# A hybrid decoder layer on one core: two output-projection weight tiles loaded earlier, two converted later, and other queues for the first inputs and the last store

## The chip, the cores and the metric

The kernel runs on one core of one Trainium2 chip. The time is device microseconds (us) of one execution; the kernel before has a median of 1073.84 us in three runs (1071.54 to 1075.19). A core has a matrix engine (TensorE, PE in the profile, with PEld for its weight loads), a vector engine (VectorE, DVE), a scalar engine (ScalarE, ACT), a general engine (GpSimd, POOL) and SyncE (SP), which only starts transfers. Each engine takes its instructions in the order in which they stand in its own program, and waits where an operand isn't ready; what stands behind a waiting instruction waits with it. A transfer is started by an instruction on SP, POOL or ACT (SPq, POOLq, ACTq in the profile) and is carried out by 16 DMA engines beside them.

## The reference

One layer of a decoder runs over 512 prompt tokens and 8 x 4 sample tokens that share the weights, all in float32, with a model width of 1024 and an FFN width of 2816:

```python
x = layer_norm(ALPHA * x + 0.5 * swiglu(x, ffn1_wg, ffn1_wu, ffn1_wd), ln1_g, ln1_b)
proj = x @ w_in                                  # 1024 -> 3328
...                                              # token shift; r, w, k, v, kk, a per head; gate g
def step(s, inp):                                # RWKV-7, 8 heads of size 64, one token at a time
    r_t, w_t, k_t, v_t, kk_t, a_t = inp
    sa = einsum("bhij,bhj->bhi", s, -kk_t)
    s = s * w_t[:, :, None, :] + sa[..., None] * (kk_t * a_t)[:, :, None, :] + v_t[..., None] * k_t[:, :, None, :]
    return s, einsum("bhij,bhj->bhi", s, r_t)
...                                              # o: group norm per head, bonus term, times g -> y_rwkv
y_conv = c_b * short_conv(c_c * c_h)             # gated convolution of width 3
mix = concat([y_rwkv, y_conv]) @ w_out           # the output projection
x = layer_norm(ALPHA * x + mix, ln2_g, ln2_b)
x = layer_norm(ALPHA * x + 0.5 * swiglu(x, ffn2_wg, ffn2_wu, ffn2_wd), ln3_g, ln3_b)
```

## The kernel before

**Layout and number form.** Activations lie transposed: 128 partitions by 8 blocks (the 1024 features) by 544 tokens, the tokens in two halves of 256 and 288 columns. A float32 product is made of three products in a shorter form (fp32r): each operand is split into a high part and a rest, and `mm3` multiplies high by high, high by rest and rest by high into one accumulator. `xhl` holds the split activations.

**Weights.** A tile of 128 x 1024 weights is brought by `wload`: SP starts a transfer of 512 KB into a `raw` buffer (line 130), ACT copies it as the high part into an `hl` buffer (line 147), and DVE subtracts to get the rest (line 148). The text calls the last two the conversion. Around the output projection there are two `raw` buffers, used in turn, so a load has to wait until the tile two places before it is converted; `hl` has eight buffers there.

**Stages.** FFN 1, layer norm, the input projection with the preparation of the recurrence, the recurrence, the output projection, layer norm, FFN 2, layer norm, store. Generators of work are woven into one another by the kernel's author's tables (`weave`, `drain`); a scheduler then puts each engine's instructions in order, by priorities that follow the order of the code. `tc.issue_after(ins)` makes what is emitted inside it stand behind `ins`.

**Ahead of the recurrence.** The recurrence is worked in 8 chunks of 64 tokens. `elim` inverts the small triangular matrices of the chunks on DVE (tiles `De`, `AT`) and moves the result through DRAM into `XT`; SP issues these transfers (line 1044), and then those that write the convolution's result to a DRAM buffer, `ycd` (lines 843 and 844).

**The recurrence** is the function `chain`, the part between about 587 and 624 us of the profile. It makes 8 steps (c = 0 to 7), one per chunk, each for two groups of heads. One step of a group is a row of small instructions that wait for one another: matmuls on PE, a copy of their result on ACT (`W`, line 1094), matmuls with `XT`, two copies of their result, one on DVE (line 1111) and one on ACT (line 1112), into the tile `UV`, matmuls for the state, and the addition that gives the next state on DVE (line 1124). After c = 3 and c = 7, ACT copies out the outputs of four chunks (line 1135, the O copies). The loop that runs `chain` (line 1373) also has ACT start four transfers that bring the residual `z` back from DRAM (`xsp`, line 1376), one for each pair of blocks. Ahead of it, SP starts two loads of 1088 KB that bring the convolution's result, split, into the blocks 4 to 7 of `xhl` (line 1369).

**The output projection** is `wout`. Its weights are eight tiles: four for the convolution's rows of `w_out`, called c0 to c3 here (`wo_c`), and four for the recurrence's rows, r0 to r3 (`wo_r`). All are loaded by `wload` at lines 1403 and 1404, in the code behind the chain; the scheduler puts some of it into gaps of the chain. Behind the chain, `gnorm` normalizes the recurrence's output in the first token half, one group of heads after the other, and splits it into the blocks 0 to 3 of `xhl` (`AO` in the profile is the output's tile, `gq` a scratch tile), beside `wout` of c0 to c3; then `wout` of r0 to r3 follows. The weights of FFN 2 (`gu`, from `in_gu`) come next.

**The start.** The first weights come in parts (`first_w`, line 713) and the first token half of the input in blocks (`first_x`, line 717), each put on SP's queue in the order in which the 96 first matmuls need them (`first_rows`, accumulators `sm`). ACT begins with an activation that loads its function table (line 704).

**The end.** The last layer norm (`layer_norm` with `to_y_last`) scales two blocks at a time and stores them; the blocks 6 and 7 are stored one by one (line 265), the others in pairs.

Of the kernel before, what the change touches and what calls it, by code (L numbers as in the profile page):

```python
# [14 lines left out]
AF = mybir.ActivationFunctionType  # L15
# [47 lines left out]
def body(ctx: ExitStack, tc: tile.TileContext, xT, gu1, wd1, win, wo_c, wo_r, gu2, wd2, lora, vec, cst,  # L63
         sst, cstate, s0, y_o, wkvp_o, wkvs_o, shift_o, conv_o):
    nc = tc.nc
    ACT, DVE, POOL = nc.scalar, nc.vector, nc.gpsimd
    dma = nc.sync.dma_start
# [26 lines left out]
    epsf, epsl, epsg, one = (eps[:, i:i + 1] for i in range(4))  # L94
# [104 lines left out]
    def drain(*fill):  # L199
        bg.extend(fill)  # L200
        take(1e9)
# [5 lines left out]
    def layer_norm(z, h, gcol, bcol, epsv, q, rs, s1, sink, pair=True, table=None):  # L207
        c0, c1 = HALF[h]
        n = c1 - c0
        end = sink is to_y_last  # L210
        m = sm()
        PE.matmul(m[:, :n], ones, s1[:, :n], start=True, stop=False)
        PE.matmul(m[:, :n], ones, z[:, KD - 1, c0:c1], start=False, stop=True)
        yield 800
        v = sm() if not pair else None
        del squares[:]
        for j in range(4):
            zz = z[:, 2 * j:2 * j + 2, c0:c1]
            qq = q[:, 2 * j:2 * j + 2, :n]
            DVE.tensor_tensor(zz, zz, m[:, None, :n].to_broadcast([P, 2, n]), op=OP.subtract)  # L220
            squares.append(ACT.activation(qq, zz, AF.Square))  # L221
            if j == 0 and table == "ahead":
                tab = issue(squares[-1], ACT.preload_act_table_set, "natural_log_exp_and_others")
            if not pair and table == "late":
                continue
            if not pair:
                yield 900
                if end and j > 1:
                    DVE.tensor_tensor(qq[:, 0, :], qq[:, 0, :], qq[:, 1, :], op=OP.add)
                nq = 1 if end and j > 1 else 2  # L230
                for i in range(nq):
                    PE.matmul(v[:, :n], ones, qq[:, i, :], start=(j == 0 and i == 0), stop=(j == 3 and i == nq - 1))
            else:
                if j % 2:
                    DVE.tensor_tensor(q[:, 2 * j - 2:2 * j, :n], q[:, 2 * j - 2:2 * j, :n], qq, op=OP.add)
                yield 900
        if not pair and table == "late":
            for j in range(4):
                yield 900
                for i in range(2):  # L240
                    PE.matmul(v[:, :n], ones, q[:, 2 * j + i, :n], start=(j == 0 and i == 0), stop=(j == 3 and i == 1))
        if pair:
            v = sm()
            for i, j in enumerate((0, 1, 4, 5)):
                PE.matmul(v[:, :n], ones, q[:, j, :n], start=(i == 0), stop=(i == 3))
        yield 800
        if table == "late":
            tab = issue(ACT.activation(warm, v[:, 0:1], AF.Copy), ACT.preload_act_table_set, "natural_log_exp_and_others")
        ln = ACT.activation(rs[:, :n], v[:, :n], AF.Ln, bias=epsv)
        if table:  # L250
            after(ln, tab)
        ACT.activation(rs[:, :n], rs[:, :n], AF.Exp, scale=-0.5)
        yield 1200
        if end:
            for d in range(0, KD, 2):
                zz = z[:, d:d + 2, c0:c1]
                DVE.tensor_tensor(zz, zz, rs[:, None, :n].to_broadcast([P, 2, n]), op=OP.mult)
                for e in (d, d + 1):
                    x, g, b = z[:, e, c0:c1], col(gcol, e), col(bcol, e)
                    if e in (3, 7):  # L260
                        DVE.tensor_scalar(x, x, g, b, op0=OP.mult, op1=OP.add)
                    else:
                        ACT.activation(x, x, AF.Identity, scale=g, bias=b)  # L263
                    if d == KD - 2:
                        dma(y_o[:, e, c0:c1], x)
                if d < KD - 2:
                    dma(y_o[:, d:d + 2, c0:c1], zz)
                yield 1200
            return
        for d in range(KD):  # L270
            zz = z[:, d, c0:c1]
            DVE.scalar_tensor_tensor(zz, zz, col(gcol, d), rs[:, :n], op0=OP.mult, op1=OP.mult)
            sink(d, zz, col(bcol, d), c0, c1)
            yield 800
# [426 lines left out]
    POOL.memset(one, 1.0)  # L701
    f1 = Ffn(z, gu1, wd1, "1", 2)
    f1.open()
    ACT.activation(warm, one, AF.Silu)
    POOL.memset(cpb[:, 0:256], 0.0)
    firsts = [sm() for _ in range(4)]
    for _ in range(4):
# [3 lines left out]
    def first_w(i, a, b):  # L711
        raw, hl = ws[i]
        dma(raw[:, a * P:b * P], gu1[i // 2, :, i % 2, a * P:b * P])  # L713
        wsplit(hl, raw, a * P, b * P)

    def first_x(a, b, c0, c1):
        dma(z[:, a:b, c0:c1], xT[:, a:b, c0:c1])
        split(xhl[:, 0, a:b, c0:c1], xhl[:, 1, a:b, c0:c1], z[:, a:b, c0:c1])

    for a, b in ((0, 2), (2, 4), (4, 8)):  # L720
# [291 lines left out]

    PLP = [(pl, par) for pl in range(4) for par in range(2)]

    def elim(XT, DM):
        est = ExitStack()
        ep = pool(est, "elim")
        AT = ep.tile([P, 32, 32], F32, name="AT")
        De = ep.tile([P, 32, 32], F32, name="De")
        tm = ep.tile([P, 256], F32, name="tm")  # L1020
        dma(AT, Ad.rearrange("a c b s t -> (a c b) s t"))
        POOL.memset(De, 0.0)
        POOL.memset(De.rearrange("p a b -> p (a b)")[:, 0:1024:33], 1.0)
        POOL.memset(XT, 0.0)
        yield 3000
        for k in range(31):
            n = 31 - k
            tv = tm[:, :n * (k + 1)].rearrange("p (i j) -> p i j", j=k + 1)
            DVE.tensor_tensor(tv, AT[:, k, k + 1:32, None].to_broadcast([P, n, k + 1]),  # L1029
                              De[:, k, None, 0:k + 1].to_broadcast([P, n, k + 1]), op=OP.mult)  # L1030
            DVE.tensor_tensor(De[:, k + 1:32, 0:k + 1], De[:, k + 1:32, 0:k + 1], tv, op=OP.add)  # L1031
            if k in (22, 30):
                a, b = (0, 24) if k == 22 else (24, 32)
                dma(Dd[0].rearrange("a c s t -> (a c) s t")[:, a:b], De[0:P:2, a:b])
                for par in range(2):
                    dma(DM[64 * par + a:64 * par + b].rearrange("p c d t -> p (c d) t"),
                        Dd[0][par, :, a:b].rearrange("c s t -> s c t"))
            yield 550
        DVE.tensor_copy(AT, De.rearrange("p a b -> p b a"))
        dma(Dd[1].rearrange("a c b s t -> (a c b) s t"), AT)  # L1040
        B = lambda par, b: slice(64 * par + 32 * b, 64 * par + 32 * b + 32)
        for b in (1, 0):
            for par in range(2):
                dma(XT[B(par, b)].rearrange("p c d t -> p (c d) t")[:, :, 32 * b:32 * b + 32],
                    Dd[1][par, :, b].rearrange("c s t -> s c t"))
        est.close()
        yield 6000
        for rnd in range(2):
            for c0 in range(0, 8, 4):
                qs = sm(), sm()  # L1050
                for c in range(c0, c0 + 4):
                    for pl, par in PLP:
                        o = ((c - c0) * 4 + pl) * 32
                        a, b = B(par, rnd), B(par, 1 - rnd)
                        if rnd:
                            lhs, rhs = DM[a, c, pl, :], XT[a, c, pl, 32:64]
                        else:
                            lhs, rhs = SC[a, pl, par, c, 32:64], DM[a, c, pl, :]
                        PE.matmul(qs[par][b, o:o + 32], lhs, rhs, start=True, stop=True)
                for par in range(2):  # L1060
                    b = B(par, 1 - rnd)
                    dst = XT[b, c0:c0 + 4, :, 32:64] if rnd else DM[b, c0:c0 + 4]
                    src = qs[par][b].rearrange("p (c d t) -> p c d t", c=4, d=4)
                    (ACT.copy if par else DVE.tensor_copy)(dst, src)
                    if rnd == 0:
                        POOL.tensor_copy(SC[R(par), :, par, c0:c0 + 4, 0:64], UV[R(par), :, par, c0:c0 + 4, :])
                yield 0
# [4 lines left out]
    def v4(q, rows=slice(0, P)):  # L1072
        return q[rows, :256].rearrange("p (d t) -> p d t", d=4)

    end = [None]

    def chain(XT, tl):
        qo, SP, W = [None] * 2, [None] * 2, [None] * 2
# [51 lines left out]
        def outputs(g, c):  # L1130
# [1 line left out]
                end[0] = PE.matmul(out(g, par, pl, c), UV[:, 2 * g + pl, par, c, :],  # L1132
                                   SC[:, 2 * g + pl, par, c, 64:128], start=(c == 0 and pl == 0), stop=True, skip_group_check=True)
            if c % 4 == 3:
                ACT.activation(O[:, 2 * g:2 * g + 2, c - 3:c + 1, :],
                               qo[g].rearrange("p (c d t) -> p d c t", c=4, d=2), AF.Copy)

        values(0, 0)
# [211 lines left out]
    pinned[0] = False  # L1350
    weave("e0", islice(el, max(0, 33 - steps[0])))
    drain()
    pinned[0] = True
    next(el)
    next(el)
# [43 lines left out]
            yield 6 * 120  # L1399

    KC, KR = (4, 5, 6, 7), (0, 1, 2, 3)
    wstate["hl"] = 0
    wc = [wload(wo_c[i]) for i in range(4)]
    wr = [wload(wo_r[i]) for i in range(4)]
    bg.append(wout(wc, KC, 0))
    with tc.issue_after(end[0].ins):
# [114 lines left out]
```

## Time and profile before

| | |
|---|---|
| median of three runs | 1073.84 us (1071.54 to 1075.19) |
| the profiled execution, its own time | 1073.96 us |
| first to last instruction in it (span) | 1072.2 us |
| mean granted clock of TensorE | 0.990 |
| bytes moved | 144.00 MB, 134 GB/s in the mean |

The page's second part cuts the span in 40 slices of 26.8 us; a digit is the busy share of a slice in tenths, 9 being 90% or more. TensorE's row and the row of the clock that it was granted:

```profile
PE   8999999999999999999999699999999999999996
PEclk9999999999999999999999799999999999999998
```

Three slices stand out in the first row: the first, the last, and the 23rd (590 to 617 us, the recurrence), which is also the one with the lowest clock. The fourth part follows the work that ended last backwards from the last instruction, and gives the shares of what it met:

```profile
PE 84%; DMA 6%; issue 5%; ACT 2%; DVE 2%; SPq 1%; ACTq 0%; POOL 0%; POOLq 0%; DVEq 0%
```

In rows of the timeline the columns are start and duration in us, engine, line, operation, output <- input, and in square brackets the engine's idle time just before, with what ended it. In groups of transfers they are the engine that started them, count, KB of each, and the median time from issue to landing in us.

### The profile page before, as it was taken

What the parts mean: (1) busy time and instruction counts of PE and PEld (TensorE: products, weight loads), DVE (VectorE), ACT (ScalarE), POOL (GpSimd) and SP (SyncE); (2) the same over time, 40 slices, a digit from 0 to 9 for tenths busy, and PEclk for the clock granted to TensorE, in tenths of its full rate; (3) what the DMA queues carried; (4) which work ended last, traced back from release to release, by engine and by line L of the source; (5) the groups of instructions that cost most, each with busy time, mean ns of one, the idle gap of its engine ahead of it and who ended that gap; (6) DMA issues with size and microseconds to landing.
All of it is one profiled execution on the core that took longest, in us unless ns stands there. A gap on an engine that the chain in (4) does not pass through costs nothing.

```text
span 1072.2 us, 22082 instructions
## 1 busy us (share of the span) xinstructions
PE 1047.8 (98%) x8960; PEld 1017.0 (95%) x8960; DVE 832.6 (78%) x1525; ACT 565.0 (53%) x1020; POOL 205.3 (19%) x300
## 2 busy tenths in 40 slices
PE   8999999999999999999999699999999999999996
PEld 8999999999999999999989599999999999999995
DVE  6788888889776766887696377788889798897655
ACT  6655555454544457665323364466555646555514
POOL 0122131212100024343213310001312122031000
PEclk9999999999999999999999799999999999999998
DMA  8658596775945131122525630243957759496302
GB/s 283 143 116 182 121 211 154 160 182 116 222 108 172 59 115 60 46 75 75 167 89 139 243 105 28 94 116 78 213 143 161 190 121 220 124 188 162 107 1 84
DMA packets 79087, 144.00 MB, mean 134 GB/s; under 512 B 16520, under 2 KB 40520, under 8 KB 78728
## 3 DMA queue, kind: packets, MB, share of 16 engines
q1 hardware_dynamic: 51208, 104.17, 29.6%
q0 software_dynamic: 27200, 36.18, 21.9%
q10 hardware_dynamic: 576, 2.23, 0.5%
q8 instruction: 70, 1.15, 0.4%
q14 instruction: 33, 0.27, 0.1%
HBM read 124.37 MB, written 9.28 MB: 125 GB/s over the span
## 4 chain that ended last, share of the span: by engine, by line
PE 84%; DMA 6%; issue 5%; ACT 2%; DVE 2%; SPq 1%; ACTq 0%; POOL 0%; POOLq 0%; DVEq 0%
PE mm L76 54%; PE sm L76 29%; DMA raw<-in_gu 3%; DMA raw<-in_wo_c 2%; ACT hl L147 1%; DMA z<-in_xT 1%; DVE hl L148 1%; DMA AT<-Ad 1%; DMA raw<-in_wo_r 0%; SPq L713 0%; DVE tm L1029 0%; DVE De L1031 0%; ACT z L263 0%; DMA Ad<-SC 0%; ACT hlb L151 0%
## 5 line engine op out<-in xcount | busy, mean ns | idle before, releaser
L76 PE MATMUL mm<-xhl,hl 128*128 128x256 f32 (+2 forms) x2640 | 362.2, 293 | 0.0
L76 PEld LDWEIGHTS mm<-xhl,hl 128*128 128x128 f32 x2640 | 342.0, 188 | 7.6 <-issue 1.4
L148 DVE TENSOR_TENSOR hl<-raw,hl 128x1024 fp32r<-128x1024 f32 (+3 forms) x224 | 261.2, 1170 | 70.1 <-ACT hl L147 69.4
L147 ACT ACTIVATE hl<-raw 128x1024 fp32r<-128x1024 f32 (+3 forms) x224 | 224.4, 1012 | 82.2 <-DVE raw L501 31.5
L76 PE MATMUL sm<-xhl,hl 128*128 128x272 f32 (+1 forms) x1392 | 194.5, 290 | 1.6 <-ACT xhl L151 1.3
L76 PEld LDWEIGHTS sm<-xhl,hl 128*128 128x128 f32 x1392 | 182.7, 190 | 2.7 <-ACT xhl L151 1.5
L76 PE MATMUL mm<-tv,hl 128*128 128x272 f32 x864 | 120.9, 289 | 0.8 <-ACT cpb L595 0.8
L76 PE MATMUL mm<-hhl,hl 128*128 128x272 f32 (+2 forms) x792 | 119.3, 294 | 0.0
L76 PEld LDWEIGHTS mm<-tv,hl 128*128 128x128 f32 x864 | 113.4, 188 | 1.5 <-ACT cpb L595 1.5
L76 PEld LDWEIGHTS mm<-hhl,hl 128*128 128x128 f32 x792 | 106.0, 188 | 4.8 <-ACT sv L641 1.5
L76 PE MATMUL sm<-hhl,hl 128*128 128x272 f32 (+2 forms) x792 | 109.7, 288 | 0.0
L76 PEld LDWEIGHTS sm<-hhl,hl 128*128 128x128 f32 x792 | 103.0, 188 | 0.5
L507 POOL DMA_DIRECT2D raw<-in_gu x36 | 43.5, 1209 | 255.2 <-DVE cpb L597 79.9
L513 POOL DMA_DIRECT2D raw<-in_wd x32 | 39.3, 1468 | 267.8 <-DVE hlb L152 232.6
L76 PE MATMUL mm<-tv,hlb 128*128 128x272 f32 x432 | 61.1, 291 | 0.0
L76 PEld LDWEIGHTS mm<-tv,hlb 128*128 128x128 f32 x432 | 56.5, 188 | 1.5 <-ACT cpb L604 1.4
L151 ACT ACTIVATE hhl<-hk 128x272 fp32r<-128x272 f32 (+1 forms) x56 | 29.5, 526 | 37.6 <-DVE hk L571 16.6
L152 DVE TENSOR_TENSOR hlb<-raw,hlb 128x512 fp32r<-128x512 f32 x52 | 35.7, 686 | 5.3 <-ACT hlb L151 5.3
L221 ACT ACTIVATE lnq<-z 128x512 f32<-128x512 f32 (+1 forms) x24 | 15.1, 656 | 46.5 <-DVE z L220 46.4
L152 DVE TENSOR_TENSOR hhl<-hk,hhl 128x272 fp32r<-128x272 f32 (+1 forms) x56 | 31.3, 558 | 6.9 <-ACT hhl L151 6.9
L501 DVE TENSOR_TENSOR raw<-raw 128x512 f32<-128x512 f32 x52 | 35.8, 688 | 1.0
L76 PE MATMUL mm<-hhl,hlb 128*128 128x272 f32 (+2 forms) x264 | 36.5, 288 | 0.0
(296 smaller groups left out, 1310.9 us busy)
## 6 DMA issues: line engine op xcount, KB each, us to landing
raw<-in_gu SPq DMA_DIRECT2D x84, 512.0 KB, 4.7
raw<-in_gu POOLq DMA_DIRECT2D x36, 512.0 KB, 6.4
raw<-in_wd SPq DMA_DIRECT2D x32, 512.0 KB, 4.4
raw<-in_win SPq DMA_DIRECT2D x26, 512.0 KB, 3.5
raw<-in_wd POOLq DMA_DIRECT2D x32, 256.0 KB, 6.5
raw<-in_wd SPq DMA_DIRECT2D x16, 384.0 KB, 3.0
z<-cpb POOLq DMA_DIRECT2D x16, 272.0 KB, 9.3
z<-sv POOLq DMA_DIRECT2D x16, 272.0 KB, 7.1
```

The lines of the kernel that those rows point to most:

```text
L76: ins = f(*args, **kw)
L147: ACT.activation(hl[:, 0, a:b], raw[:, a:b], AF.Copy)
L148: DVE.tensor_tensor(hl[:, 1, a:b], raw[:, a:b], hl[:, 0, a:b].bitcast(F32), op=OP.subtract)
L151: ACT.activation(hi, x, AF.Copy)
L152: DVE.tensor_tensor(lo, x, hi.bitcast(F32), op=OP.subtract)
L221: squares.append(ACT.activation(qq, zz, AF.Square))
L501: DVE.tensor_tensor(y[:, :, 0], y[:, :, 1], a[:, :, 1], op=OP.add)
L507: POOL.dma_start(x.rearrange("p (s c) -> p s c", s=2), bass.AP(tensor=a11.tensor, offset=a11.offset, ap=[[2 * D, P], [P * 2 * D, 2], [1, 5 ...
L513: POOL.dma_start(four(x)[:, i], bass.AP(tensor=a11.tensor, offset=a11.offset, ap=[[DFF, P], [P * DFF, 2], [1, 256]]), accum_op=OP.add)
```

## The change

There are three edits.

The first concerns c0 to c3. c0 and c1 are now loaded right behind the last DVE instruction of `elim` (`end[2]`), in the code well ahead of the chain; c2 and c3 only behind the last O copy (`end[1]`). r0 to r3 follow them in the code as before.

The second concerns the start. The first token half of the input blocks 0 to 3 is loaded by three transfers that ACT starts, two of them ahead of its table load and one behind it; SP no longer loads them. The table load now comes behind `first_w` in the code.

The third: of the last two stores of the last layer norm, that of block 6 is started by ACT.

```diff
@@ layer_norm
                     if d == KD - 2:
-                        dma(y_o[:, e, c0:c1], x)
+                        (dma if e in (3, 7) else ACT.dma_start)(y_o[:, e, c0:c1], x)
@@ the start
     f1.open()
-    ACT.activation(warm, one, AF.Silu)
     POOL.memset(cpb[:, 0:256], 0.0)
...
+    for k in range(2):
+        ACT.dma_start(z[:, k:k + 1, 0:256], xT[:, k:k + 1, 0:256])
+    ACT.activation(warm, one, AF.Silu)
+    ACT.dma_start(z[:, 2:4, 0:256], xT[:, 2:4, 0:256])
+
     def first_x(a, b, c0, c1):
-        dma(z[:, a:b, c0:c1], xT[:, a:b, c0:c1])
+        if a >= 4 or c0:
+            dma(z[:, a:b, c0:c1], xT[:, a:b, c0:c1])
         split(xhl[:, 0, a:b, c0:c1], xhl[:, 1, a:b, c0:c1], z[:, a:b, c0:c1])
@@ elim
+    end = [None] * 3
+
     def elim(XT, DM):
...
-        DVE.tensor_copy(AT, De.rearrange("p a b -> p b a"))
+        end[2] = DVE.tensor_copy(AT, De.rearrange("p a b -> p b a"))
...
-    end = [None]
@@ chain, outputs
             if c % 4 == 3:
-                ACT.activation(O[:, 2 * g:2 * g + 2, c - 3:c + 1, :],
+                end[1] = ACT.activation(O[:, 2 * g:2 * g + 2, c - 3:c + 1, :],
                                qo[g].rearrange("p (c d t) -> p d c t", c=4, d=2), AF.Copy)
@@ ahead of the chain's loop
     drain()
+    wstate["hl"] = 0
+    with tc.issue_after(end[2].ins):
+        wc = [wload(wo_c[i]) for i in range(2)]
     pinned[0] = True
@@ behind the chain's loop
     KC, KR = (4, 5, 6, 7), (0, 1, 2, 3)
-    wstate["hl"] = 0
-    wc = [wload(wo_c[i]) for i in range(4)]
+    with tc.issue_after(end[1].ins):
+        wc += [wload(wo_c[i]) for i in range(2, 4)]
     wr = [wload(wo_r[i]) for i in range(4)]
```

In the rows below, a name with its number is one buffer's use. On ScalarE, around steps 3 and 4 of the chain before (`W0` and `W1` are the two groups' W; the conversions of the tiles c1 and c2 are `hl_7761` and `hl_7766`):

```order
L1112 COPY UV_4724<-sm_7359 64x2x64
L1112 COPY UV_4724<-sm_7371 64x2x64
L147 ACTIVATE hl_7761<-raw_7760 128x1024
L1094 ACTIVATE W0_7406<-sm_7401 128x128
L1094 ACTIVATE W1_7420<-sm_7415 128x128
L1112 COPY UV_4724<-sm_7426 64x2x64
L147 ACTIVATE hl_7766<-raw_7765 128x1024
L1112 COPY UV_4724<-sm_7438 64x2x64
L1135 ACTIVATE AO_4715<-mm_7227 128x2x256
L1135 ACTIVATE AO_4715<-mm_7228 128x2x256
```

On ScalarE in the changed kernel, from step 1 of the chain on (c1 is `hl_7042` here), and then, behind the dots, from the chain's last copy on (c2 and c3 are `hl_7766` and `hl_7771`):

```order
L1100 ACTIVATE W0_7283<-sm_7278 128x128
L147 ACTIVATE hl_7042<-raw_7041 128x1024
L1100 ACTIVATE W1_7297<-sm_7292 128x128
L1118 COPY UV_4724<-sm_7303 64x2x64
L1118 COPY UV_4724<-sm_7315 64x2x64
L1385 DMA z_7233<-xsp_72 128x1088 x2
...
L1118 COPY UV_4724<-sm_7718 64x2x64
L1141 ACTIVATE AO_4715<-mm_7479 128x2x256
L1141 ACTIVATE AO_4715<-mm_7480 128x2x256
L147 ACTIVATE hl_7766<-raw_7765 128x1024
L147 ACTIVATE hl_7771<-raw_7770 128x1024
```

The conversion of c1 moved from step 3 to step 1, between the two groups' W; that of c2 from between the two groups' copies of step 3 to behind the chain, where c3's follows it. On SyncE before, from the last transfers into `ycd` to the stores of the final states (`out_wkvp`):

```order
L844 DMA ycd_73<-zc_6479 128x544
L843 DMA ycd_73<-cu_6865 128x544
L844 DMA ycd_73<-zc_6866 128x544
L1363 DMA out_conv<-cvo_4294 128x72
L130 DMA raw_7760<-in_wo_c 128x1024
L1369 DMA xhl_68<-ycd_73 128x4x544 x2
L130 DMA raw_7765<-in_wo_c 128x1024
L130 DMA raw_7770<-in_wo_c 128x1024
L130 DMA raw_7775<-in_wo_r 128x1024
L1128 DMA out_wkvp<-W0_7720 128x128
L1128 DMA out_wkvp<-W1_7734 128x128
```

And on SyncE now, from the same transfer on:

```order
L849 DMA ycd_73<-zc_6479 128x544
L130 DMA raw_7041<-in_wo_c 128x1024
L848 DMA ycd_73<-cu_6865 128x544
L849 DMA ycd_73<-zc_6866 128x544
L1372 DMA out_conv<-cvo_4294 128x72
L130 DMA raw_7765<-in_wo_c 128x1024
L1378 DMA xhl_68<-ycd_73 128x4x544 x2
L130 DMA raw_7770<-in_wo_c 128x1024
L1134 DMA out_wkvp<-W0_7730 128x128
L1134 DMA out_wkvp<-W1_7744 128x128
L130 DMA raw_7775<-in_wo_r 128x1024
```

c1 (`raw_7760` before, `raw_7041` now) went ahead of two transfers into `ycd`, c2 (`raw_7765`) ahead of the `xhl` loads, and the first tile of `wo_r` behind the stores of the states. At the start, SyncE's queue before:

```order
L717 DMA z<-in_xT 128x256
L713 DMA raw<-in_gu 128x256
L717 DMA z<-in_xT 128x256
L713 DMA raw<-in_gu 128x256 x4
L717 DMA z<-in_xT 128x2x256
L713 DMA raw<-in_gu 128x256 x3
L713 DMA raw<-in_gu 128x512
L717 DMA z<-in_xT 128x2x256
```

And now on SyncE (the first five rows) and, behind the dots, on ScalarE:

```order
L712 DMA raw<-in_gu 128x256 x8
L712 DMA raw<-in_gu 128x512
L722 DMA z<-in_xT 128x2x256
L712 DMA raw<-in_gu 128x512
L722 DMA z<-in_xT 128x2x256
...
L716 DMA z<-in_xT 128x256 x2
L717 ACT_TABLE_LOAD
L717 ACTIVATE warm<-eps 128x1
L718 DMA z<-in_xT 128x2x256
L151 ACTIVATE xhl<-z 128x256
L147 ACTIVATE hl<-raw 128x256
```

The three transfers of `z` for blocks 0 to 3 left SyncE's queue, so that blocks 4 and 5 are its 10th transfer instead of its 13th; on ScalarE two of them stand ahead of the table load and one behind it, all ahead of the first split.

## The prediction

> **What bounds the kernel now.** I read the page's busy shares first, then who made TensorE wait, then the stretches around the longest of those waits, and last the instructions in it, engine by engine.
>
> ```profile
> span 1072.2 us, 22082 instructions
> PE 1047.8 (98%) x8960; PEld 1017.0 (95%) x8960; DVE 832.6 (78%) x1525; ACT 565.0 (53%) x1020; POOL 205.3 (19%) x300
> ```
>
> TensorE (PE) is the bound: of 1072.2 us it is idle for 24.4. A change that leaves the matmuls alone can win only from those 24.4 us, and from time in which the clock is low. The profiled execution took 1073.96 us, which is the span and 1.76 us around it, and lies 0.12 us above the median of 1073.84.
>
> ```profile
> PE sm L76 <- ACT UV L1112: 9.0, 1, 9.0
> 599.00:608.30 9.30, 0.29 (x9) 0.15 (x4) 0.84 (x3) 1.32 (x2) 0.80 (x2) 0.61 0.75 299
> 608.30:614.80 6.50, 6.47 (x102) 5.94 (x102) 3.23 (x9) 2.16 (x6) 1.51 (x4) 0.51 0.25 83
> 614.80:624.20 9.40, 9.40 (x237) 8.57 (x234) 4.76 (x17) 3.88 (x14) 4.08 (x11) 1.00 0.01 3
> ```
>
> The first row is a wait (total, times, longest): once, for 9.0 us, a matmul waited for ScalarE's copy at L1112. The others are stretches (length, busy time of PE, PEld, DVE, ACT and POOL, granted clock, DMA share, GB/s). PE stands still from 599 to 608.3, and in the next 6.5 us it is busy at a clock of 0.51, after which it is 1.00. So the hole costs more than its length. What ScalarE (ACT) did:
>
> ```profile
> 590.01 0.28 ACT L1094 ACTIVATE W<-sm 128x128 f32<-128x128 f32 x1 [1.28 <-PE sm L76]
> 593.40 0.28 ACT L1094 ACTIVATE W<-sm 128x128 f32<-128x128 f32 x1 [1.24 <-PE sm L76]
> 596.63 0.28 ACT L1094 ACTIVATE W<-sm 128x128 f32<-128x128 f32 x1 [0.22 <-PE sm L76]
> 606.94 1.06 ACT L147 ACTIVATE hl<-raw 128x1024 fp32r<-128x1024 f32 x1 [8.89 <-DMA raw<-in_wo_c]
> 609.98 0.27 ACT L1094 ACTIVATE W<-sm 128x128 f32<-128x128 f32 x1
> 615.00 0.28 ACT L1094 ACTIVATE W<-sm 128x128 f32<-128x128 f32 x1 [2.02 <-PE sm L76]
> 618.16 0.28 ACT L1094 ACTIVATE W<-sm 128x128 f32<-128x128 f32 x1 [1.25 <-PE sm L76]
> 621.34 0.28 ACT L1094 ACTIVATE W<-sm 128x128 f32<-128x128 f32 x1 [1.25 <-PE sm L76]
> ...
> 577.72 0.63 SPq L844 DMA_DIRECT2D ycd<-zc  x1
> 588.04 0.44 SPq L130 DMA_DIRECT2D raw<-in_wo_c  x1
> 589.25 1.27 SPq L1369 DMA_DIRECT2D xhl<-ycd  x2
> 590.57 0.83 SPq L130 DMA_DIRECT2D raw<-in_wo_c  x1
> xhl<-ycd SPq DMA_DIRECT2D x2, 1088.0 KB, 13.6
> L1376 ACTq DMA_DIRECT2D z<-xsp x4: 326/343/1207, 590.6 to 594.2; - x4
> ```
>
> The seven L1094 rows are W of the first head group in steps 1 to 7 of the recurrence: steps of 3.39, 3.23, **13.35**, **5.02**, 3.16 and 3.18 us. In the long one ACT idles 8.89 us ahead of converting c2 (the third `wo_c` tile), whose load was issued at 590.57 behind both `xhl` loads (1088 KB each, 13.6 us to landing) and beside the four `z` loads (last row: their triggers' shortest, median and longest time in ns, and when the first and the last was). The chain's own copy at L1112 stands behind that conversion. The 5.02 us step is the one at half clock.
>
> **The chain, part one: what goes.** c2 and c3 are now converted behind the chain's last O copies, so no instruction of the chain stands behind their landing. Steps 3 and 4 shrink to the mean of the two clean ones, 3.17: 13.35 + 5.02 - 2 x 3.17 = **12.0 us** off. Nothing I find takes its place: c1 is issued behind the transfer of 577.72, so at about 578.4, and has until 590.3 to land; c2 takes the queue place that c1 had at 588.04; `xhl`, landed by about 605, is wanted only by the products behind the chain, which now ends near 613.
>
> **The chain, part two: what is added.**
>
> ```profile
> 591.87 0.28 DVE L1111 COPY UV<-sm 64x128 f32<-64x128 f32 x1 [0.37 <-PE sm L76]
> L148 DVE TENSOR_TENSOR hl<-raw,hl x22: 1210/1219/1434, 510.6 to 696.6; 128x1024 fp32r<-128x1024 f32 x22
> ```
>
> c1's conversion moves from step 3 (where its cost goes with the 13.35) into step 1. ACT's half takes 1.06 us from 590.29, between the two W copies; VectorE's half is queued ahead of the second group's UV copy and can start at 591.50, when the first group's copy ends (0.37 idle before 591.87). At the median of 1.22 us for such a conversion, the second group's copy starts at 592.72 instead of 591.87, and behind it stand the updates that step 2 needs: **+0.85**. The four `z` triggers stay inside the chain, two steps of it, as before; the longest took 1.21 us, the median 0.34. I count them at nothing more; if two more take 1.21, that is +1.7. Chain: -12.0 + 0.85 = **-11.2 us**, between -12.0 (c1 hidden) and -9.4 (both).
>
> **Behind the chain: the `wo_r` loads.** Two raw buffers serve all eight tiles. r0 used to be loaded during the chain; now it waits for c2's conversion behind it, so all four come one place later.
>
> ```profile
> 626.89 6.12 SPq L130 DMA_DIRECT2D raw<-in_wo_r  x3
> 635.05 4.71 SPq L130 DMA_DIRECT2D raw<-in_gu  x2
> raw<-in_wo_r SPq DMA_DIRECT2D x3, 512.0 KB, 4.0
> 638.24 0.42 ACT L1262 ACTIVATE gq<-gq 128x256 f32<-128x256 f32 x1
> 639.76 0.42 ACT L151 ACTIVATE xhl<-AO 128x256 fp32r<-128x256 f32 x1 [1.11 <-DVE AO L1270]
> 641.59 0.41 DVE L1270 TENSOR_TENSOR AO<-gq,sm 128x256 f32<-128x256 f32 x1
> 642.49 0.43 DVE L152 TENSOR_TENSOR xhl<-AO,xhl 128x256 fp32r<-128x256 f32 x1 [0.48 <-ACT xhl L151]
> 642.51 0.73 PE L76 MATMUL mm<-xhl,hl 128*128 128x256 f32 x3
> ```
>
> On the clock of the execution before (the chain ends at 623.9 there), r0, r1, r2 take the times of r1, r2, r3, so only r3 is new: it takes the place of the `gu` load at 635.05, lands at 639.05 by the median of 4.0, is converted by ACT until 640.1 (the idle time before 639.76 covers 1.1 us) and by VectorE until 641.3. On VectorE six instructions stand behind it before the last normalized block is ready (0.42 + 0.42 + 0.48 + 0.42 + 0.48 + 0.41, 2.2 with their overlap): that product ends at 643.5 instead of 642.0, and its split at about 644.7 instead of 642.92. PE uses that split right away (642.51 and on), with no slack; the new order puts about 0.7 us of other matmuls ahead of it. **+1.0 us**, between 0 (landing 1.0 us sooner than the median) and +2.5 (1.5 us later).
>
> **The start.**
>
> ```profile
> 4.40:12.40 8.00, 7.92 (x50) 7.20 (x48) 4.19 (x10) 3.79 (x10) 0.00 (x0) 1.00 0.82 247
> 12.40:14.40 2.00, 0.44 (x2) 0.24 (x2) 1.49 (x3) 1.70 (x4) 0.00 (x0) 1.00 1.07 392
> 14.35 5.83 PE L76 MATMUL sm<-xhl,hl 128*128 128x256 f32 x47 [0.34 <-DVE xhl L152]
> 6.44 0.43 SPq L717 DMA_DIRECT2D z<-in_xT  x1
> 12.94 0.63 ACT L151 ACTIVATE xhl<-z 128x512 fp32r<-128x512 f32 x1
> 2.87 0.42 ACT L151 ACTIVATE xhl<-z 128x256 fp32r<-128x256 f32 x1 [0.63 <-DMA z<-in_xT]
> ```
>
> PE needs 5.83 us for 47 of the 96 first matmuls, and resumes at 14.35 when `z` blocks 4 and 5, issued at 6.44 as SyncE's 13th transfer, are split. Three transfers leave SP's queue ahead of them; at 0.47 us each (0.43 and a gap) that is 1.4 us, and DMA share 0.82 leaves room before 12.4. ACT pays for three triggers: its first split moves from 2.87 to about 3.6, but weights land at 3.4 to 3.9, so the first matmul stays near 4.4. **-1.4 us**. Bounds: -4.0 (9.95 us from 4.40 to 14.35 spent on 49 matmuls that need 6.1 at that pace) and +1.0 (triggers of 1.21 us on ACT). I take the value nearest SP's own rows.
>
> The Trainium skill speaks against this edit ("DMA: Bandwidth & Descriptors", Issuing engines are not separate DMA queues): transfers started by different engines run on the same 16 DMA engines, and starting them from several engines saves only the sequencer's time. By that rule the sum has at most these 1.4 us, and 0 where the engines are full. The share of 0.82 agrees with the first; from 12.4 on, 1.07 agrees with the second.
>
> **The end.**
>
> ```profile
> DMA  0000000000000000007999999999960000000000
> 1068.08 0.92 SPq L265 DMA_DIRECT2D out_y<-z  x2
> ```
>
> The last two stores are issued one behind the other; now ACT issues one, 0.46 us saved at most. But the digits (40 slices of 1062 to 1073) show the DMA engines at 90% or more from 1067.2 to 1070.2 without a gap: the last bytes wait for earlier stores, not for the trigger. **-0.1**, between 0 and -0.46.
>
> **Sum**: -11.2 + 1.0 - 1.4 - 0.1 = -11.7; 1073.96 - 11.7 = **1062.3 us**.
>
> **Rivals.**
>
> ```profile
> DMA to landing us min/median/max: 2.0/3.3/15.7
> raw<-in_gu SPq DMA_DIRECT2D x4, 256.0 KB, 6.8
> ```
>
> The first row is the view of the tile `ycd`, whose longest transfers are the `xhl` loads; the second, weights at the start.
>
> - *The start is bound by bytes.* Then ACT's triggers only reorder transfers: -11.2 + 1.0 - 0.1, **1063.7 us**. For it: share 1.07 from 12.4; against: 0.82 before.
> - *The `wo_r` loads become the bound.* If r0 and r2, two loads in series in one buffer, take the 6.8 us of loads at the start instead of 4.0, twice 2.8 us more, PE waits some 5 us where I counted 1.0: **1066.3 us**. Against: behind the chain nothing else loads.
> - *The hole only moves.* c1 lands after 590.3, or another wait stops ACT as long: the chain saves nothing, **1073.5 us**. Against: it has 11.9 us for 512 KB.
> - *Slower:* ACT's first `z` trigger, now in step 1 behind two loads more of SP's, waits until both `xhl` loads have landed. The place is the head of step 2; landing at up to 605.6 (the second is issued some 0.6 into the 1.27, at 589.9, and 15.7 later) it would stop the chain at 592.5 for 13 us, restart it at half clock (2.6 us), and keep the +1.0: 1.9 us later than now with the start's gain, **1075.9 us**, and above 1077 without it. It decides from a landing of about 604 on. Against: before, the triggers went from 590.6 on, with both `xhl` loads (issued from 589.25 on) still in flight.
>
> **How the numbers follow.** Forecast 0.64, bytes at the start 0.16, `wo_r` 0.11, moved hole 0.05, slower 0.04. Runs of one kernel differ by 0.3%, some 3.2 us, so that is the bound for no change: faster 0.91; same 0.06 (the moved hole and a part of the last case); slower 0.03. The range takes the chain to -12.0 and the start toward -2.5 at the low end with run spread (1058.5), and the `wo_r` case at the high end (1067); outside lie the last two cases and tails.
>
> **What would show it.** Right: no ACT wait for `in_wo_c` in the chain; seven W copies within about 20.1 us; clock 1.00 from 588 to 613; a short PE wait for the split of the second group's last block some 19 us behind the chain; PE's 96 first matmuls over near 18.6; the last bytes as late behind the last activation as now. Wrong: a new idle stretch of PE over 3 us, a clock near 0.5 anywhere, or `z` triggers of several us on ACT.

## The result, and the profile after

The changed kernel takes 1061.82 us in the median (1060.83 to 1062.75, four runs), the kernel before 1073.88 us (1071.54 to 1075.19, four runs): a ratio of 0.989 with a 95% interval of 0.9871 to 0.9909. The forecast was 1062.3 us. Two later groups of runs, each with the kernel before beside it, gave 0.9904 (0.9867 to 0.9942) and 0.9902 (0.9882 to 0.9923), so the gain is 10.5 to 12 us. In the profiled executions the span went from 1072.2 to 1061.0 us.

The page's head and TensorE's busy shares:

```profile
span 1061.0 us, 22077 instructions
PE 1045.9 (99%) x8960; PEld 1014.1 (96%) x8960; DVE 832.0 (78%) x1525; ACT 564.6 (53%) x1020; POOL 204.7 (19%) x300
```

TensorE is now idle for 15.1 us instead of 24.4, and busy 1.9 us less with the same 8960 matmuls. The half clock that went fits this: in steps 3 and 4 alone it is busy 6.6 us instead of 9.0. Who made it wait (total in us, times, longest):

```profile
PE sm L76 <- ACT lnq L221: 1.4, 1, 1.4
PE sm L76 <- POOL cpb L704: 1.2, 1, 1.2
PE mm L76 <- ACT cpb L595: 0.6, 2, 0.4
PE sm L76 <- issue: 0.5, 1, 0.5
PE sm L76 <- DVE X L1201: 0.4, 1, 0.4
PE mm L76 <- ACT xhl L151: 0.4, 1, 0.4
PE sm L76 <- DVE UV L1117: 0.4, 1, 0.4
```

The 9.0 us behind the copy into `UV` are gone. Two rows are new: 0.5 with the releaser "issue", a wait for nothing that the profile shows, and 0.4 for a split of `xhl`. ScalarE in the chain, with the first group's W of steps 1 to 7 and the conversions:

```profile
588.74 0.28 ACT L1100 ACTIVATE W<-sm 128x128 f32<-128x128 f32 x1 [1.28 <-PE sm L76]
588.91 1.05 ACT L147 ACTIVATE hl<-raw 128x1024 fp32r<-128x1024 f32 x1
592.67 0.28 ACT L1100 ACTIVATE W<-sm 128x128 f32<-128x128 f32 x1 [1.65 <-PE sm L76]
595.89 0.28 ACT L1100 ACTIVATE W<-sm 128x128 f32<-128x128 f32 x1 [1.30 <-PE sm L76]
599.14 0.28 ACT L1100 ACTIVATE W<-sm 128x128 f32<-128x128 f32 x1
602.67 0.28 ACT L1100 ACTIVATE W<-sm 128x128 f32<-128x128 f32 x1 [1.50 <-PE sm L76]
606.34 0.28 ACT L1100 ACTIVATE W<-sm 128x128 f32<-128x128 f32 x1 [1.75 <-PE sm L76]
609.52 0.28 ACT L1100 ACTIVATE W<-sm 128x128 f32<-128x128 f32 x1 [1.25 <-PE sm L76]
612.73 2.00 ACT L147 ACTIVATE hl<-raw 128x1024 fp32r<-128x1024 f32 x2
```

The steps are 3.93, 3.22, 3.25, 3.53, 3.67 and 3.18 us where they were 3.39, 3.23, 13.35, 5.02, 3.16 and 3.18. From W of step 1 to W of step 7 that is 20.78 instead of 31.33 us. No conversion of c1 to c3 waits for its load: c1's stands in step 1, those of c2 and c3 run behind the chain. The steps 1, 4 and 5 as stretches (length, busy time of PE, PEld, DVE, ACT and POOL, granted clock, DMA share, GB/s):

```profile
588.74:592.67 3.93, 3.46 (x85) 2.91 (x86) 2.73 (x8) 1.91 (x5) 1.29 (x4) 1.00 0.83 285
599.14:602.67 3.53, 3.38 (x85) 2.96 (x85) 1.63 (x6) 1.08 (x6) 1.55 (x4) 1.00 1.03 412
602.67:606.34 3.67, 3.22 (x85) 2.86 (x85) 1.74 (x7) 1.07 (x5) 2.00 (x5) 1.00 0.24 94
```

The clock is 1.00 in all three, as from 588 to 613 us as a whole. Of what is left over 3.2 us, 0.47 in step 1 and 0.45 in step 5 are idle time of PE; in steps 1 and 4 it is also busy for 0.2 to 0.3 more than those 3.2. At the start, two rows before and five now:

```profile
4.46 7.90 PE L76 MATMUL sm<-xhl,hl 128*128 128x256 f32 x48
20.01 1.23 PE L76 MATMUL mm<-xhl,hl 128*128 128x288 f32 x8
```

```profile
4.00 0.42 ACT L151 ACTIVATE xhl<-z 128x256 fp32r<-128x256 f32 x1 [0.82 <-DMA z<-in_xT]
4.78 7.17 PE L76 MATMUL sm<-xhl,hl 128*128 128x256 f32 x49
12.29 2.32 PE L76 MATMUL sm<-xhl,hl 128*128 128x256 f32 x13 [0.34 <-DVE xhl L152]
14.83 4.33 PE L76 MATMUL sm<-xhl,hl 128*128 128x256 f32 x34 [0.22 <-DVE hl L148]
19.00 1.23 PE L76 MATMUL mm<-xhl,hl 128*128 128x288 f32 x8
```

PE resumes 2.06 us sooner than before (12.29 instead of 14.35), but it began 0.3 later, and waits a second time, for weights, at 14.83. The next work, which began at 20.01 before, begins at 19.00.

### The profile page after: what moved, and what is told of

It reads as the page before. It is cut to its first block, busy times and chain, and to the rows that moved or that the text cites. A ratio compares the mean times of both kernels' runs of the same rounds, so it can differ in the third digit from the quotient of the medians.

```text
span 1061.0 us, 22077 instructions
## 1 busy us (share of the span) xinstructions
PE 1045.9 (99%) x8960; PEld 1014.1 (96%) x8960; DVE 832.0 (78%) x1525; ACT 564.6 (53%) x1020; POOL 204.7 (19%) x300
## 3 DMA queue, kind: packets, MB, share of 16 engines
q8 instruction: 70, 1.15, 0.4%
## 4 chain that ended last, share of the span: by engine, by line
PE 84%; DMA 5%; issue 5%; DVE 3%; ACT 3%; SPq 0%; POOL 0%; POOLq 0%; DVEq 0%; ACTq 0%
PE mm L76 55%; PE sm L76 29%; DMA raw<-in_gu 4%; ACT hl L147 2%; DMA raw<-in_wo_r 1%; DVE hl L148 1%; DMA AT<-Ad 1%; DVE tm L1036 0%; DVE De L1038 0%; ACT z L263 0%; DMA Ad<-SC 0%; ACT hlb L151 0%; SPq L712 0%; POOL SP L1104 0%; DVE zc L828 0%
## 5 line engine op out<-in xcount | busy, mean ns | idle before, releaser
L221 ACT ACTIVATE lnq<-z 128x512 f32<-128x512 f32 (+1 forms) x24 | 15.1, 656 | 46.5 <-DVE z L220 46.4
```

## Experiments

A table of all profiles first, since most points are read from three stretches: when the first matmul with 288 columns begins (the end of the start), from W of step 1 to W of step 7, and from there to the end of the span. "Issue" is TensorE's wait for nothing that the profile shows, in the chain. All in us.

| kernel | end of start | W1 to W7 | W7 to end | issue | median, runs |
|---|---|---|---|---|---|
| before | 20.01 | 31.33 | 450.9 | 0 | 1073.88, 4 |
| start edit only | 19.02 | 30.80 | 451.2 | 0 | 1073.36, 10 |
| changed, first profile | 19.00 | 20.78 | 451.5 | 0.5 | 1061.82, 4 |
| changed, second | 19.31 | 21.49 | 452.1 | 1.3 | 1064.08, 4 |
| changed, third | 18.74 | 21.03 | 451.8 | 0.8 | 1062.88, 6 |
| weight edit only | 19.72 | 22.03 | 451.6 | 1.8 | 1064.08, 4 |
| only deferred | 19.78 | 20.94 | 452.2 | 1.0 | 1064.17, 7 |
| only early | 18.98 | 21.45 | 451.7 | 0.7 | 1063.78, 4 |
| without the start edit | 19.53 | 21.47 | 451.0 | 1.2 | 1064.10, 6 |
| z spread | 18.77 | 20.25 | 455.2 | 0 | 1063.29, 4 |
| c1 ahead | 19.11 | 21.15 | 451.5 | 1.5 | 1062.98, 1 |
| c1 behind | 19.12 | 20.87 | 452.3 | 0.9 | 1063.48, 1 |
| c1 ahead, z spread | 19.40 | 19.88 | 451.5 | 0.3 | 1062.23, 5 |

The medians come from three groups of runs, in which the kernel before took 1073.01, 1074.79 and 1073.35 us; only the ratios given below compare across groups.

**The first edit alone.** The kernel before with the diff's parts on `wc`, without those on the start and the last store.

> Only the first edit (c0 and c1 loaded ahead, c2 and c3 converted behind the chain); the start and the last store as before. My theory: the chain loses its hole and the half clock behind it, so that from W of step 1 to the chain's end it takes 23.4 us as in the changed kernel instead of 33.9 (-10.5), and the tail gives back 0.6 through the wo_r loads: 1073.9 - 9.9 = 1064.0 us. Rival, that the start edit gives nothing and all of the gain is here: 1061.9 us.

1064.08 us, a ratio of 0.9908 (0.9892 to 0.9925): the first edit alone carries the gain within the uncertainty of the comparison. Its chain took 22.03 us, 1.3 more than in the first profile of the changed kernel. So much larger is its "issue" (1.8 instead of 0.5), most of it one wait in step 5:

```profile
607.71 0.45 PE L76 MATMUL sm<-UV,SC 128*64 128x64 f32 x8 [1.50 <-issue]
```

**The second edit alone.**

> Only the second edit (the first three input transfers by ScalarE). My theory, that SyncE's queue set the start: the work up to the recurrence comes 1.3 us sooner as in the changed kernel, PE resumes near 12.3 instead of 14.35, and the time is 1072.6 us, with the hole of 9 us still there. Rival, that bytes set it: first stage as long as before, 1073.9 us.

1073.36 us, a ratio of 1.0006 (0.9992 to 1.0019): no gain that the runs can tell. In its profile TensorE begins the 96 first matmuls at 5.49 us, runs through them without a wait, and comes to the next work at 19.02. The hole is as it was:

```profile
PE sm L76 <- ACT UV L1117: 9.1, 1, 9.1
```

The hole is here with the start edit and without it, so the start has no part in it.

**Which half of the first edit removes the hole?** Two kernels: one in which only c2 and c3 are deferred, one in which only c0 and c1 come early. Both are the kernel before with one of these pieces:

```diff
 # only deferred: at the place behind the chain
-    wc = [wload(wo_c[i]) for i in range(4)]
+    wc = [wload(wo_c[i]) for i in range(2)]
+    with tc.issue_after(end[1].ins):
+        wc += [wload(wo_c[i]) for i in range(2, 4)]
 # only early: the piece ahead of the chain as in the change, and behind it
+    wc += [wload(wo_c[i]) for i in range(2, 4)]
```

> Of the first edit only the second half: c2 and c3 behind the chain's last O copies; c0 and c1 as before, so that c1 is loaded at about 588 and converted at the end of step 2. My theory, that the hole is a conversion waiting in the chain and its deferral alone removes it: 1064.0 us, within 0.7 of the kernel with the whole first edit, no wait of ScalarE for in_wo_c over 1 us. Rival, that the early load of c1 is needed too: c1's conversion now waits in the chain for a load beside xhl and z, 1067 to 1070 us with a wait of 3 us or more.

> Of the first edit only the first half: c0 and c1 loaded ahead, while c2 and c3 stay free of the chain's end, so that c2's load stands ahead of both xhl loads and its conversion inside step 3, between the two groups' W. My theory, that the hole was the late landing behind xhl and not the place of the conversion: c2 lands within 7 us of its issue, its conversion costs the chain 0.5 to 0.9 as c1's does, r0 comes in time: 1063.5 to 1065 us. Rival, that all transfers share the same engines and c2 lands near 600 all the same: a stall of 4 to 5 us, a stretch at half clock, 1068 to 1070 us.

1064.17 us, ratio 0.9931 (0.9909 to 0.9953), and 1063.78 us, ratio 0.991 (0.9895 to 0.9925). In both profiles the hole is gone, and the intervals don't separate one half from both together. But the runs with deferral alone agree less. Four took 1063.1 to 1064.2 us at a mean granted clock of 0.997 to 0.998; three took 1067.2, 1067.7 and 1071.2 us at 0.995, 0.995 and 0.992, where all runs with early loads have 0.997 or 0.998. In this kernel c1 is still loaded late, at 586.7 us, and converted in the chain, so a part of the hole may have come back in those three; none of them was profiled, and this is not shown.

In the kernel with early loads, c2's conversion stands in step 3:

```profile
595.38 0.28 ACT L1095 ACTIVATE W<-sm 128x128 f32<-128x128 f32 x1 [1.30 <-PE sm L76]
595.56 1.05 ACT L147 ACTIVATE hl<-raw 128x1024 fp32r<-128x1024 f32 x1
596.50 0.27 ACT L1095 ACTIVATE W<-sm 128x128 f32<-128x128 f32 x1
```

It waits for nothing: issued ahead of the two `xhl` loads, c2 had landed. So the hole was the queue place of a load whose conversion stood in the chain; the rival, that all loads land equally late on shared engines, falls. The price of the place is seen too: step 3 took 4.16 us here (595.38 to 599.54), 3.25 in the changed kernel. Little of it is left a step later: steps 3 and 4 together took 7.2 us, against 6.8 to 7.4 in the three profiles of the changed kernel.

**The changed kernel again**, beside the next kernels.

> The changed kernel again, on the chip of this group, to be set against the kernel with only the first edit (ratio 0.9908 to before). Theory one, that the start edit is worth the 1.3 us by which the two first traces differ: ratio 0.989 to 0.990 (11 to 12 us). Theory two, that the start of the kernel before varies by 1 us from run to run and the edit gives about half a microsecond at most: ratio 0.990 to 0.9915 (9 to 10.5 us).

A ratio of 0.9904 (0.9867 to 0.9942), whose interval covers both expectations: inconclusive. The wait in step 5 was 0.9 us in its profile, and 0.4 more came in step 4.

**The new wait of TensorE.** The changed kernel with the `z` loads tied to later copies of the chain:

```diff
-            ACT.copy(state(g, 1, c), v2(qs[1], R(1)))
+            lastcopy[0] = ACT.copy(state(g, 1, c), v2(qs[1], R(1)))
...
-            ACT.dma_start(z[:, k:k + 2, :], xsp[:, k:k + 2, :])
+            after(ACT.dma_start(z[:, k:k + 2, :], xsp[:, k:k + 2, :]), lastcopy[0])
```

> The changed kernel with the four z loads spread over the chain (behind the copies of steps 1, 2, 4 and 6, instead of two steps). My theory of the new wait of TensorE in step 5 (0.45 to 1.5 us, released by nothing that the profile shows): the transfers that bring TensorE's own instructions stand behind data on full DMA engines, so with the engines less full after about 597 the wait is gone (under 0.2 us) and steps 4 to 7 take 3.2 us each: chain 0.5 to 1 us shorter than in the changed kernel, 1061 to 1062.5 us. Rival, that these transfers have a pace of their own: the same wait of 0.4 to 1.5 us at the same instruction. Second rival, that the last z pair lands after it is wanted: a new wait behind the chain of 1 us or more.

The wait is gone. The steps 4, 5 and 6 as stretches of this kernel, and steps 4 and 5 of the changed kernel's second profile, in the same columns as above:

```profile
598.11:601.65 3.54, 3.41 (x84) 2.95 (x84) 1.67 (x6) 1.07 (x5) 1.54 (x4) 1.00 0.94 330
601.65:604.83 3.18, 3.18 (x84) 2.91 (x84) 1.71 (x7) 1.07 (x4) 1.59 (x4) 1.00 0.43 148
604.83:608.01 3.18, 3.18 (x85) 2.91 (x84) 1.71 (x7) 1.07 (x4) 1.59 (x4) 1.00 0.17 23
```

```profile
599.40:603.15 3.75, 3.34 (x84) 2.95 (x84) 1.66 (x6) 1.07 (x5) 1.55 (x4) 1.00 1.02 408
603.15:607.32 4.17, 3.23 (x85) 2.87 (x85) 1.75 (x7) 1.08 (x5) 2.41 (x7) 1.00 0.30 117
```

Step 5 is 3.18 instead of 4.17 us. The chain took 20.25 us, 0.5 to 1.2 less than the three profiles of the changed kernel; step 4 stayed at 3.5, where 3.2 was expected. The median is 1063.29 us, above the 1061 to 1062.5 expected, and a ratio of 0.9898 (0.9867 to 0.993) where the changed kernel had 0.9904 in the same group: such an amount is below what the runs resolve. The long stretch behind the chain (455.2) is seen only in this profile, of the slowest of the four runs (1064.99): it has a wait of 1.2 us on `cpb` in FFN 2, around 800 to 840 us, with a clock of 0.96 in those 40 us.

**The price of c1's conversion in step 1.** The changed kernel with the conversion tied to the idle time of both engines ahead of step 1, and one with it behind the chain:

```diff
 # c1 ahead (conv1: the two halves of c1's conversion)
+   after(conv1[0], u)      # ACT: behind the last copy of step 0
+   after(w, conv1[0])      # ... ahead of W of step 1
+   after(conv1[1], u)      # DVE: behind the updates of step 0
+   after(u, conv1[1])      # ... ahead of the first copy of step 1
 # c1 behind
-        wc = [wload(wo_c[i]) for i in range(2)]
+        wc = [wload(wo_c[0])]
...
-        wc += [wload(wo_c[i]) for i in range(2, 4)]
+        wc += [wload(wo_c[i]) for i in range(1, 4)]
```

> The changed kernel with c1's conversion pulled out of step 1: ScalarE's half between step 0's copies and W of step 1, VectorE's half between step 0's updates and step 1's first copy, where both engines are idle for 1.1 to 1.3 us. My theory, that the conversion costs what it takes between the copies: step 1 falls from 3.93 to 3.2 to 3.4 us. Rival, that step 1 is long for another reason (the first state addition by GpSimd, the DMA engines): still 3.8 to 4.0.

> The changed kernel with c1 converted behind the chain too, so that every load from c3 on comes one more place later. My theory, that each place costs about as much as its load and conversion once the slack behind the chain is used up (the first place cost 0.4 us of waiting): step 1 takes 3.2 us (-0.7), TensorE waits 2.5 to 4 us behind the chain, 1063 to 1066 us. Rival, that the loads behind the chain are hidden: TensorE waits under 0.5 us there and the time falls by the 0.7 of step 1.

Each of these kernels ran once, so only their profiles are read. With c1 ahead, step 1 took 3.45 us (588.57 to 592.02, W to W), with c1 behind 3.39; in the changed kernel 3.93. So the conversion costs 0.5 us. My expectation of the second kernel failed on its larger part: every load from c3 on comes one more place later, and TensorE waits no longer for it. Its one wait behind the chain (from 611 us on):

```profile
PE mm L76 <- ACT xhl L151: 0.4, 1, 0.4
```

0.4 us, as much as in the changed kernel, where 2.5 to 4 were expected: in this profile the loads behind the chain have slack for two places. The stretch from W7 to the end is 452.3 us, against 451.5 to 452.1 in the changed kernel.

**Start, and both cures together.** A yardstick, the changed kernel without the start edit, and one with c1 ahead and `z` spread.

> The changed kernel, as the yardstick of this group: 1062 to 1064 us, with a wait of TensorE for nothing that the profile shows of 0.4 to 1.5 us in step 5 or 6 of the chain in its profile.

> The changed kernel without the start edit (inputs of blocks 0 to 3 by SyncE again, table load first). Theory one, the prediction's: the start is worth 1.3 us or more, so this kernel is 1.3 us slower than the changed one in this group, 1063.5 to 1065.5. Theory two: the old start varies from run to run and ends at 18.9 to 20.0 us against 18.8 to 19.3 for the new one, so the difference is 0.3 to 0.8 us, which the runs of this group hardly resolve; W of step 1 comes within 0.8 us of the changed kernel's in the profiles' mean.

> The changed kernel with both cures of what is left in the chain: c1's conversion out of step 1 and the z loads spread over the chain. My theory: step 1 at 3.4 instead of 3.9 us, no wait in steps 5 and 6, W of step 1 to W of step 7 within 19.9 us where the changed kernel takes 20.8 to 21.5; 1 us faster than the changed kernel in this group (0.5 to 1.7). Rival, that the wait for instructions only moves to another place of the chain or behind it: no gain.

Ratios to before: 0.9902 (0.9882 to 0.9923), 0.9913 (0.9891 to 0.9934) and 0.9887 (0.987 to 0.9905). The yardstick's profile has its wait of 0.8 us in step 4, where step 5 or 6 was expected. The medians of the first two are 1.2 us apart, between the two theories, with intervals that overlap for the most part. The profiles decide better. The five kernels with the old start end it at 20.01, 19.72, 19.78, 18.98 and 19.53 us (mean 19.60), the eight with the new one between 18.74 and 19.40 (mean 19.06): some 0.5 us, and the profile of the kernel before was the slowest of its kind. The third kernel has the shortest chain of all, 19.88 us, with 0.3 us of "issue" left; its median is 0.65 us below the changed kernel's, the lowest of the group, though not separated from it.

The last store's edit was not run alone. The profiles answer it: from the start of VectorE's last instruction to the end of the span, before and changed (rows of the timeline):

```profile
1067.12 0.41 DVE L261 TENSOR_SCALAR z<-z,vc 128x256 f32<-128x256 f32 x1
```

```profile
1055.88 0.41 DVE L261 TENSOR_SCALAR z<-z,vc 128x256 f32<-128x256 f32 x1
1056.84 0.34 ACTq L265 DMA_DIRECT2D out_y<-z  x1
1057.14 0.34 SPq L265 DMA_DIRECT2D out_y<-z  x1
```

1072.2 - 1067.12 = 5.1 us, and 1061.0 - 1055.88 = 5.1 us.

## Why the prediction was right, step by step

**The hole.** Right in place, mechanism and size. Steps 3 and 4 went from 18.37 to 6.78 us, 11.6 off where 12.0 were predicted. The size itself varies: in the profile of the start edit alone the same two steps, hole and all, took 17.5 us, since less half clock followed. The kernels with one half of the edit show that a load in a late queue place, with its conversion in the chain, made it.

**c1 in step 1.** Right mechanism, too large a size: 0.85 was predicted, 0.5 is what three kernels show (3.93 against 3.39 with it behind the chain and 3.45 with it ahead).

**"Nothing I find takes its place."** This sentence failed. TensorE's wait for instructions took a part of the hole's place: 0.5 to 1.8 us in the profiles of all kernels without the hole and with the `z` loads in two steps, none with the hole, and none or 0.3 with the `z` loads spread. It is a small case of the rival of the moved hole, from a cause that I hadn't listed; the profile before could not show it, since the standstill came first.

**The `wo_r` loads.** The place was right, with a size of 0.4 instead of 1.0. The last split of the second group, the one named:

```profile
627.08 1.06 ACT L147 ACTIVATE hl<-raw 128x1024 fp32r<-128x1024 f32 x1 [0.50 <-DMA raw<-in_wo_r]
632.12 0.43 DVE L152 TENSOR_TENSOR xhl<-AO,xhl 128x256 fp32r<-128x256 f32 x1 [0.48 <-ACT xhl L151]
632.14 1.20 PE L76 MATMUL mm<-xhl,hl 128*128 128x256 f32 x8 [0.37 <-ACT xhl L151]
```

From the chain's end (612.1) it is finished 20.4 us later, where it was 19.0 before: 1.4 later instead of the 1.8 predicted, and PE's other work covered all but 0.37. The prediction's own figures give 1.5: its product ends at 643.5, and the split took 0.92 from there, which makes 644.4 and not 644.7. The stretch from W7 to the end grew by 0.6 in the pair of first profiles.

**The start.** The step that was mis-sized most: -1.4 predicted, some -0.5 measured as a mean over profiles, nothing in the time of the kernel with that edit alone. Two parts of its working failed. The first matmul did not stay near 4.4: it began at 4.78. The first input landed later, so that its split began at 4.00 instead of 2.87, after 0.82 us of waiting; nine weight transfers were started beside it, which I take for the reason. And I named nothing that is late next: it was a weight tile, at 14.83. (The lower bound of -4.0 is -3.9 by its own figures, 9.95 less 6.1.) The Trainium skill's rule ("DMA: Bandwidth & Descriptors", Issuing engines are not separate DMA queues), that starting transfers from several engines saves only the sequencer's time, agrees with the runs: 0.5 us, less than the 1.4 us that the three triggers took. That the old start varies by 1 us between profiles (18.98 to 20.01 us) could not be seen in one.

**The end.** Predicted at -0.1, measured as 0.0 (5.1 us in both). The row of digits that the prediction read is at 90% until 1070.0, not 1070.2.

**The sum.** The pair of profiles gives -1.3 up to W of step 1, -10.55 in the chain and +0.6 behind it: -11.2, against -11.7. That it came so near is in part luck. The start's gain was sized 0.9 too large, and the costs of c1 and of the `wo_r` loads together by about as much, so these errors cancel; the wait for instructions was left out. The pair also holds a slow start of the kernel before, and an execution with more half clock than most: its mean granted clock is 0.990, where 28 of the 34 later executions of the same kernel have 0.992 to 0.994. The two later groups put the gain at 10.7 and 10.5 us.

The slower rival's mechanism did not occur: ScalarE's first `z` triggers took 0.93 us for two and stopped nothing. Its price of 1.9 us does not follow from the terms written there, either: -12.0, +13, +2.6, +1.0 and -1.5 make 3.1.

## What to carry to other kernels

A conversion that the scheduler puts into a chain of small dependent instructions costs little as long as its load has landed (c1's cost 0.5 us); look in the queue for what stands ahead of that load, since moving either the load or the conversion removed the stall in its profile. By the times of the runs, moving the load did so in all four, and doing both gained no more that these runs resolve; with the conversions alone deferred, three runs of seven took 3 to 7 us longer than the rest. When a long wait goes, ask what ran during it unseen: here it was the refill of TensorE's instructions. Where a term rests on a place that comes once in a kernel, such as its start, take several profiles of it before sizing it.

## What the runs showed of the hardware

TensorE can run out of instructions. The page's third part has a queue of instruction transfers:

```profile
q8 instruction: 70, 1.15, 0.4%
```

70 packets of 1.15 MB: TensorE's 8960 matmuls and 8960 weight loads make 17920 instructions, or 256 for each packet, so I take this queue for TensorE's. In the chain it spends some 170 instructions in a step of 3.18 us (85 and 85), which is a packet in 4.8 us. The microseconds in which a packet's transfer began:

| kernel | packets at (us) | TensorE's wait |
|---|---|---|
| changed, second profile | 585, 590, 598, 604, 607, 612 | 0.9 in step 5, 0.4 in step 4 |
| z spread | 584, 589, 596, 600, 605, 610 | none |

While the DMA engines are full (share 1.02 from 593 to 603 in the first row, 0.96 in the second) the packets come 8 and 6 us apart, and TensorE stands in step 5 until the late one; with the data spread one gap of 7 us is followed by 4 and 5, and nothing waits.

Two things in the traces tie the wait to the packets. TensorE stands for "issue" in the chain in ten of the profiles, 13 times in all: always at one of the same two places in its order of matmuls and weight loads, and these are 256 instructions apart, which is one packet. And each time it goes on 1.25 to 1.52 us after the end of a packet's transfer. In the changed kernel's second profile the packet that starts at 604.27 takes 1.06 us, and 1.44 us later:

```profile
606.77 0.45 PE L76 MATMUL sm<-UV,SC 128*64 128x64 f32 x8 [0.94 <-issue]
```

Why the packet comes late is less sure. The transfers of the late packets took 1.0 to 1.1 us, no longer than others, so the delay lies ahead of their start. That they stood behind data on the same engines fits both rows; the queueing itself was not seen.

The Trainium skill ("Runtime: NRT & Kernel Launch", Instruction fetch mechanics) says that the sequencer fetches blocks of 16 KiB, 256 instructions, through a DMA queue of its own while it runs the present one, at a cost mostly hidden. The size agrees (1.15 MB / 70 = 16.4 KB); the cost does not in this chain, with 0.5 to 1.8 us of waiting where the `z` loads come in two steps.

The half clock behind a hole comes in pieces of 3.41 us, as far as these traces show. Its records last 13.65 us in the kernel before, 10.24 with the start edit alone, and 3.41 in FFN 2 of the kernel with `z` spread: 4, 3 and 1 times 3.41. So a hole of the same 9 us was followed by 6.4 us at half clock in the first profile and 3.7 in the second, and step 4 took 5.02 and 4.04 us.
